# Decay sums masked and exponentiated in the tile they are loaded into, loads issued three ticks sooner

## The chip, the cores and the metric

The kernel runs on one core of a Trainium2 chip, in one launch. The metric is the time of the device for one execution, in microseconds, as a median over runs. TensorE is called PE, VectorE DVE, ScalarE ACT, GpSimd POOL and SyncE SP, as in the profile.

## The reference

One layer for 128 context and 1024 latent tokens, width 1024. Two branches, a Fourier one and a state-space one (SSD), are merged, projected and added to the input. The change touches the SSD branch only, whose core the reference writes like this (once forward and once on the flipped sequence):

```python
xdt = xf * dtf
acs = jnp.cumsum(da, axis=-1)                      # decay sums, within chunks of 128
seg = acs[..., :, None] - acs[..., None, :]
lmat = jnp.exp(jnp.where(tri, seg, -jnp.inf))
y_diag = jnp.einsum("bclgn,bcsgn,bgrcls,bcsgrp->bclgrp", cc, bc, lmat, xdt)
decay_states = jnp.exp(acs[..., -1:] - acs)
chunk_states = jnp.einsum("bcsgn,bgrcs,bcsgrp->bcgrpn", bc, decay_states, xdt)
...
final, states_in = lax.scan(step, s0, (chunk_states, chunk_decay))
y_off = jnp.einsum("bclgn,bcgrpn,bgrcl->bclgrp", cc, states_in, jnp.exp(acs))
y = y_diag + y_off
```

There are 32 heads of 64 channels in 8 groups of 4 heads that share B and C (128 wide), and 9 chunks of 128 tokens: chunk 0 is the context, 1 to 8 are the latents.

## The kernel before

Everything is float32, held transposed (channels on partitions, tokens along the free axis). The large products are done in three matmuls of a high and a low part (`mm3`, L101 to L103); `split` makes these parts: a cast on ACT for the high one (L89), a subtraction on DVE for the low one (L79).

The SSD phase, from about 130 us to 1100 us, is a loop over the 8 groups `g`. A group projects its B, x and C chunks, `GATES[g]` gate chunks and its z chunks, each a `gemm` of 3 token tiles by 8 steps by 3 matmuls of 128x384. Beside them run small steps: transposes, the states and the outputs. The order on PE is written by hand: `at(step, ticks)` puts the next piece of a generator at a tick of a clock, and `gemm` advances this clock by one every 6 matmuls. The other engines' order, SP's queue of DMA issues included, is made by a scheduler from the program and its buffers. Each engine takes its instructions in that order, and a tile of a ring (`tag`, `bufs`) is written again only after all work on its former content.

`states(g, k)` weighs x with DVE (`xw`), splits it into `xhl`, and a yield later runs the `st` matmuls: the first matmul of each needs the high part, the second the low part. For k = -1 the result, the context's final state, goes by ACT's copy `so` (L557) to DRAM; k = 0 to 6 carry the scan on (`st`). `outputs(g, c)` runs once per chunk, in the order 0, 4, 5, 3, 6, 2, 7, 1, 8. SP loads the decay sums of 4 heads and both directions, broadcast to 128 partitions, 512 KB, from `d_acs` (L572) into `ab`; POOL masks them into `e` by two selects (L582, L583), ACT takes 8 exps in `e` (L586), DVE adds the directions (L587). A yield later PE does C times B (`cb`, L590) and DVE multiplies it into `e`; another yield later come the matmuls `po` (from the states) and `y` (L605, from `e`), and DVE adds both into `xs`.

Before, `xhl` and `e` share the tag "e" with three tiles, `ab` and `so` the tag "ab" with two. Loads of an output are six ticks ahead of its `y` in the program, `cb` three; `st` of `k` stands at tick 21 + 3k from its base, and the outputs' clock base is 12 ticks later. In the text, st_3 and xhl_3 mean k = 3, while e_4 or y_0 name the chunk c.

Of the kernel before, what the change touches and what calls it, by code (L numbers as in the profile page):

```python
# [12 lines left out]
F32 = mybir.dt.float32  # L13
F32R = mybir.dt.float32r
AF = mybir.ActivationFunctionType
ALU = mybir.AluOpType
# [46 lines left out]
def tile_step(ctx, tc, a, o):  # L63
# [127 lines left out]
    def at(step, *ticks):  # L191

        for t in ticks:
            events[clock[0] + t].append(step)
# [281 lines left out]
    with pool("sd") as sd, pool("ss") as ss, pool("sx", side="right") as sx:  # L476
# [65 lines left out]
        def states(g, k, xb, bn, sts):  # L542

            cf, cb = (0, 0) if k < 0 else (1 + k, 8 - k)
            xw = ss.tile([P, 2, 256], F32, tag="xw", name=f"xw{g}_{k}", bufs=1)
            xhl = ss.tile([P, 2, 2, 256], F32R, tag="e", name=f"xhl{g}_{k}", bufs=3)
            xh, xl = xhl[:, 0], xhl[:, 1]
            for d, c in ((0, cf), (1, cb)):
                tt(xw[:, d].rearrange("p (j h q) -> p j h q", j=2, h=2), xb[:, c].rearrange("p (j h q) -> p j h q", j=2, h=2),
                   wsv[:, c, d, g, :].rearrange("p (h j) -> p j h", h=2).unsqueeze(3).broadcast_to([P, 2, 2, 64]), ALU.mult)  # L550
            split(xh, xl, xw)
            yield
            ps = gps(f"st{g}_{k}")
            if k < 0:
                mm3(ps, (bn[:, 0, 0], bn[:, 1, 0]), [x.rearrange("p d q -> p (d q)") for x in (xh, xl)], True, True)
                so = ss.tile([P, 1024], F32, tag="ab", name=f"so{g}", bufs=2)[:, 0:512]
                S.copy(so, ps)  # L557
                nc.sync.dma_start(o["sout"][g], so)
                return
            st = sts[0]  # L560
            for d, c in ((0, cf), (1, cb)):
                mm3(ps[:, d * 256 : d * 256 + 256], (bn[:, 0, c], bn[:, 1, c]), (xh[:, d], xl[:, d]), True, True)
            tt(st[:, k + 1].rearrange("p d (h q) -> p d h q", h=4), st[:, k].rearrange("p d (h q) -> p d h q", h=4),
               decv[:, :, g, :, k].unsqueeze(3).broadcast_to([P, 2, 4, 64]), ALU.mult)
            sv = st[:, k + 1].rearrange("p d q -> p (d q)")
            tt(sv, sv, ps, ALU.add)

        def outputs(g, c, bt, ct, xs, xb, st):

            cc = slice(col(c), col(c) + P)  # L570
            ab = ss.tile([P, 2, 4, P], F32, tag="ab", name=f"ab{g}_{c}", bufs=2)
            nc.sync.dma_start(ab.rearrange("p d h l -> p d (h l)"),  # L572
                              d_acs[c].rearrange("(d g q) l -> g d (q l)", d=2, g=NG)[g].partition_broadcast(P))
            if c > 0:

                ea = ss.tile([P, 2, 2, P], F32, tag="ea", name=f"ea{g}_{c}", bufs=3)
                for r0 in range(2):
                    nc.sync.dma_start(ea[r0 * 64 : r0 * 64 + 64].rearrange("p d j l -> p d (j l)"),
                                      d_eac[c].rearrange("(d g h j) l -> g h d (j l)", d=2, g=NG, h=2)[g, r0].partition_broadcast(64))
            e = ss.tile([P, 2, 4, P], F32, tag="e", name=f"e{g}_{c}", bufs=3)  # L580

            G.affine_select(e[:, 0], ab[:, 0], [[0, 4], [1, P]], ALU.is_ge, -1e30, base=0, channel_multiplier=-1)  # L582
            G.affine_select(e[:, 1], ab[:, 1], [[0, 4], [-1, P]], ALU.is_ge, -1e30, base=0, channel_multiplier=1)  # L583
            for d in range(2):
                for h in range(4):
                    act(e[:, d, h], e[:, d, h], AF.Exp, bias=knv[:, c, d, g, h : h + 1])  # L586
# [56 lines left out]
        for g in range(NG):  # L643
# [12 lines left out]
                at(tr_x(g, c0, xs, xb), 11 + i)  # L656
            at(skip(g, xs), 16)
            for k in range(-1, 7):
                at(states(g, k, xb, bn, sts), 17 + 3 * k, 21 + 3 * k)
            conv_silu(C0 + g, 8 + g, ct, f"c{g}")  # L660
            st = ss.tile([P, 8, 2, 256], F32, tag="st", name=f"st{g}")
            sts.append(st)
# [1 line left out]

            for i, c in enumerate((0, 4, 5, 3, 6, 2, 7, 1, 8)):
                t = 20 + 3 * i
                at(outputs(g, c, bt, ct, xs, xb, st), t - 6, t - 3, t)
            done = clock[0] + t
            gate(GATES[g])

# [478 lines left out]
```

## Time and profile before

| | us |
|---|---|
| median of 3 runs | 1739.71 (1739.43 to 1741.41) |
| the profiled execution | 1747.27 |
| its span | 1745.1 |
| PE busy in it | 1711.1 (98%) |
| DVE, ACT, POOL busy | 1094.4, 811.2, 186.5 |

The profiled execution has 2.2 us around its span, and it is 7.6 us longer than the median. The span is cut into instructions by engine; the page gives each engine's busy time, the chain of work that ended last, and groups of instructions by line. A wait of an engine is its idle time ahead of an instruction, put down to what released it. Where the timeline shows `[1.41 <-DVE e L79]`, the engine was idle for 1.41 us and the end of DVE's line 79 on `e` let it go on.

### The profile page before, as it was taken

To read this page: it belongs to the slowest core of one execution; us is meant where nothing else is said; L and a number is where in the kernel's file an instruction comes from. 1 tells how busy PE (TensorE), PEld (TensorE's weight loads), DVE (VectorE), ACT (ScalarE), POOL (GpSimd) and SP (SyncE) were. 2 spreads that over 40 slices of the span, in tenths; PEclk is the share of its full clock that TensorE was granted. 3 is DMA by queue.
4 is the path that set the end of the run, shared out by engine and by line. 5 is a ranking of instruction groups with operands and counts; after the bars stand their busy time and mean duration, and the time that the engine had idled before them with its cause. 6 is when DMAs were issued, how large, how long until landed. Compare 5 with 4: busy or idle time off the path is not lost.

```text
span 1745.1 us, 27930 instructions
## 1 busy us (share of the span) xinstructions
PE 1711.1 (98%) x10728; PEld 1643.9 (94%) x10728; DVE 1094.4 (63%) x1875; ACT 811.2 (46%) x1667; POOL 186.5 (11%) x266
## 2 busy tenths in 40 slices
PE   6999999999999999999899999999999999999998
PEld 4999999999999999999899999999988999999987
DVE  5676866866756757757658668677587424444432
ACT  6445656665565566566466666315333211112221
POOL 0200300300300301301202103301000000000000
PEclk9999999999999999999999999999999999999999
DMA  9233632633523624524525436551066647643432
GB/s 345 78 71 95 157 94 83 150 100 88 151 83 104 146 71 114 144 76 104 122 70 142 103 105 140 195 179 54 3 212 217 221 145 235 220 168 125 160 121 72
DMA packets 110136, 229.63 MB, mean 132 GB/s; under 512 B 20594, under 2 KB 56436, under 8 KB 108340
## 3 DMA queue, kind: packets, MB, share of 16 engines
q1 hardware_dynamic: 108708, 223.14, 42.9%
q0 software_dynamic: 1296, 4.72, 0.7%
q8 instruction: 84, 1.38, 0.3%
q14 instruction: 48, 0.39, 0.1%
HBM read 187.24 MB, written 40.58 MB: 131 GB/s over the span
## 4 chain that ended last, share of the span: by engine, by line
PE 91%; DVE 4%; DMA 3%; ACT 1%; issue 1%; SPq 0%; POOL 0%; DVEq 0%; POOLq 0%; ACTq 0%
PE mm_g L101 5%; PE mm_g L103 5%; PE mm_g L102 5%; PE mm_x L101 4%; PE mm_x L103 4%; PE mm_x L102 4%; PE mm_z L101 3%; PE mm_z L103 3%; PE mm_z L102 3%; PE po L597 3%; PE y L605 2%; PE mm_c L101 2%; PE mm_c L103 2%; PE o L102 2%; PE mm_c L102 2%; PE o L103 2%
## 5 line engine op out<-in xcount | busy, mean ns | idle before, releaser
L73 ACT ACTIVATE e<-e,kwN 128x128 f32<-128x128 f32 x576 | 179.5, 390 | 114.4 <-POOL e L582 108.5
L101 PE MATMUL mm_g<-hT,wh_g 128*128 128x384 f32 x528 | 182.0, 345 | 0.0
L103 PE MATMUL mm_g<-hT,wl_g 128*128 128x384 f32 x528 | 177.9, 337 | 0.0
L102 PE MATMUL mm_g<-hT,wh_g 128*128 128x384 f32 x528 | 177.5, 336 | 0.0
L101 PE MATMUL mm_z<-hT,wh_z 128*128 128x384 f32 x384 | 134.1, 349 | 0.0
L582 POOL TENSOR_SCALAR_AFFINE_SELECT e<-ab 128x512 f32<-128x512 f32 x72 | 50.2, 697 | 779.4 <-PE st L103 662.0
L101 PE MATMUL mm_x<-hT,wh_x 128*128 128x384 f32 x384 | 131.6, 343 | 0.0
L103 PE MATMUL mm_z<-hT,wl_z 128*128 128x384 f32 x384 | 129.8, 338 | 0.0
L102 PE MATMUL mm_z<-hT,wh_z 128*128 128x384 f32 x384 | 129.5, 337 | 0.0
L103 PE MATMUL mm_x<-hT,wl_x 128*128 128x384 f32 x384 | 129.2, 337 | 0.0
L102 PE MATMUL mm_x<-hT,wh_x 128*128 128x384 f32 x384 | 129.0, 336 | 0.0
L101 PEld LDWEIGHTS mm_g<-hT,wh_g 128*128 128x128 f32 x528 | 99.3, 188 | 0.5 <-issue 0.2
L102 PEld LDWEIGHTS mm_g<-hT,wh_g 128*128 128x128 f32 x528 | 99.3, 188 | 0.4
L103 PEld LDWEIGHTS mm_g<-hT,wl_g 128*128 128x128 f32 x528 | 99.1, 188 | 0.0
L101 PEld LDWEIGHTS mm_z<-hT,wh_z 128*128 128x128 f32 x384 | 72.6, 189 | 0.9 <-issue 0.9
L102 PEld LDWEIGHTS mm_z<-hT,wh_z 128*128 128x128 f32 x384 | 72.6, 189 | 0.0
L101 PEld LDWEIGHTS mm_x<-hT,wh_x 128*128 128x128 f32 x384 | 72.1, 188 | 0.3
L103 PEld LDWEIGHTS mm_z<-hT,wl_z 128*128 128x128 f32 x384 | 72.3, 188 | 0.0
L102 PEld LDWEIGHTS mm_x<-hT,wh_x 128*128 128x128 f32 x384 | 72.3, 188 | 0.0
L103 PEld LDWEIGHTS mm_x<-hT,wl_x 128*128 128x128 f32 x384 | 72.1, 188 | 0.0
L597 PE MATMUL po<-ct,st 128*128 128x128 f32 x512 | 67.4, 274 | 0.0
L101 PE MATMUL mm_b<-hT,wh_b 128*128 128x384 f32 x192 | 65.8, 343 | 1.4 <-DVE gt L76 1.4
(419 smaller groups left out, 4746.9 us busy)
## 6 DMA issues: line engine op xcount, KB each, us to landing
ab<-d_acs SPq DMA_DIRECT2D x72, 512.0 KB, 5.9
ea<-d_eac SPq DMA_DIRECT2D x128, 128.0 KB, 3.6
wr_g<-in_w_in SPq DMA_DIRECT2D x24, 512.0 KB, 3.7
yr<-d_y SPq DMA_DIRECT2D x16, 576.0 KB, 4.3
aw<-in_ada_ss SPq DMA_DIRECT2D x8, 1024.0 KB, 10.2
wr_x<-in_w_in SPq DMA_DIRECT2D x16, 512.0 KB, 3.9
wr_z<-in_w_in SPq DMA_DIRECT2D x16, 512.0 KB, 3.6
d_y<-xs SPq DMA_DIRECT2D x16, 512.0 KB, 3.4
```

Of the source, the lines that this page charges most:

```text
L73: S.activation(out, in_, func, bias=bias, scale=scale, **kw)
L101: PE.matmul(ps, lhs[0], rhs[0], start=first, stop=False)
L102: PE.matmul(ps, lhs[0], rhs[1], start=False, stop=False)
L103: PE.matmul(ps, lhs[1], rhs[0], start=False, stop=last)
L582: G.affine_select(e[:, 0], ab[:, 0], [[0, 4], [1, P]], ALU.is_ge, -1e30, base=0, channel_multiplier=-1)
L597: PE.matmul(po[:, (2 * d + j) * P : (2 * d + j + 1) * P], st[:, k, d, j * P : j * P + P], ct[:, cc], start=True, stop=True)
L605: PE.matmul(py[r0 : r0 + 64, j * P : j * P + P], xb[:, c, h * 64 : h * 64 + 64], e[:, 0, h % 2 * 2 + j], start=True, stop=True, tile_posit ...
```

## The change

The separate tile `ab` is gone. The load goes into the `e` tile, where selects and exps then work in place; tag "e" has four tiles, shared by `e` and `so`. `xhl` gets a tag of its own with one tile. `outputs` has one more yield: the load stands nine ticks ahead of `y`, selects and exps six, `cb` three as before. The `st` matmuls stand one tick sooner (20 + 3k). No instruction is added or taken out but the waits; the on-chip memory is the same (five tiles of 4 KB a partition).

```diff
--- before.py
+++ after.py
@@ -543,7 +543,7 @@
 
             cf, cb = (0, 0) if k < 0 else (1 + k, 8 - k)
             xw = ss.tile([P, 2, 256], F32, tag="xw", name=f"xw{g}_{k}", bufs=1)
-            xhl = ss.tile([P, 2, 2, 256], F32R, tag="e", name=f"xhl{g}_{k}", bufs=3)
+            xhl = ss.tile([P, 2, 2, 256], F32R, tag="xhl", name=f"xhl{g}_{k}", bufs=1)
             xh, xl = xhl[:, 0], xhl[:, 1]
             for d, c in ((0, cf), (1, cb)):
                 tt(xw[:, d].rearrange("p (j h q) -> p j h q", j=2, h=2), xb[:, c].rearrange("p (j h q) -> p j h q", j=2, h=2),
@@ -553,7 +553,7 @@
             ps = gps(f"st{g}_{k}")
             if k < 0:
                 mm3(ps, (bn[:, 0, 0], bn[:, 1, 0]), [x.rearrange("p d q -> p (d q)") for x in (xh, xl)], True, True)
-                so = ss.tile([P, 1024], F32, tag="ab", name=f"so{g}", bufs=2)[:, 0:512]
+                so = ss.tile([P, 1024], F32, tag="e", name=f"so{g}", bufs=4)[:, 0:512]
                 S.copy(so, ps)
                 nc.sync.dma_start(o["sout"][g], so)
                 return
@@ -568,8 +568,8 @@
         def outputs(g, c, bt, ct, xs, xb, st):
 
             cc = slice(col(c), col(c) + P)
-            ab = ss.tile([P, 2, 4, P], F32, tag="ab", name=f"ab{g}_{c}", bufs=2)
-            nc.sync.dma_start(ab.rearrange("p d h l -> p d (h l)"),
+            e = ss.tile([P, 2, 4, P], F32, tag="e", name=f"e{g}_{c}", bufs=4)
+            nc.sync.dma_start(e.rearrange("p d h l -> p d (h l)"),
                               d_acs[c].rearrange("(d g q) l -> g d (q l)", d=2, g=NG)[g].partition_broadcast(P))
             if c > 0:
 
@@ -577,10 +577,10 @@
                 for r0 in range(2):
                     nc.sync.dma_start(ea[r0 * 64 : r0 * 64 + 64].rearrange("p d j l -> p d (j l)"),
                                       d_eac[c].rearrange("(d g h j) l -> g h d (j l)", d=2, g=NG, h=2)[g, r0].partition_broadcast(64))
-            e = ss.tile([P, 2, 4, P], F32, tag="e", name=f"e{g}_{c}", bufs=3)
-
-            G.affine_select(e[:, 0], ab[:, 0], [[0, 4], [1, P]], ALU.is_ge, -1e30, base=0, channel_multiplier=-1)
-            G.affine_select(e[:, 1], ab[:, 1], [[0, 4], [-1, P]], ALU.is_ge, -1e30, base=0, channel_multiplier=1)
+            yield
+
+            G.affine_select(e[:, 0], e[:, 0], [[0, 4], [1, P]], ALU.is_ge, -1e30, base=0, channel_multiplier=-1)
+            G.affine_select(e[:, 1], e[:, 1], [[0, 4], [-1, P]], ALU.is_ge, -1e30, base=0, channel_multiplier=1)
             for d in range(2):
                 for h in range(4):
                     act(e[:, d, h], e[:, d, h], AF.Exp, bias=knv[:, c, d, g, h : h + 1])
@@ -656,7 +656,7 @@
                 at(tr_x(g, c0, xs, xb), 11 + i)
             at(skip(g, xs), 16)
             for k in range(-1, 7):
-                at(states(g, k, xb, bn, sts), 17 + 3 * k, 21 + 3 * k)
+                at(states(g, k, xb, bn, sts), 17 + 3 * k, 20 + 3 * k)
             conv_silu(C0 + g, 8 + g, ct, f"c{g}")
             st = ss.tile([P, 8, 2, 256], F32, tag="st", name=f"st{g}")
             sts.append(st)
@@ -664,7 +664,7 @@
 
             for i, c in enumerate((0, 4, 5, 3, 6, 2, 7, 1, 8)):
                 t = 20 + 3 * i
-                at(outputs(g, c, bt, ct, xs, xb, st), t - 6, t - 3, t)
+                at(outputs(g, c, bt, ct, xs, xb, st), t - 9, t - 6, t - 3, t)
             done = clock[0] + t
             gate(GATES[g])
```

The order of instructions moves with it. In the rows that follow, a name is the tile, its group and its index, and a running number; `x8` after a shape means eight in a row.

ACT in group 3, before, from the skip's scaling of `xs3` (L73) to the exps of the group's first output (`gt67`: a gate's tiles, `wh_z`: a weight's split):

```order
L73 ACTIVATE xs3_4944<-xs3_4944,dcol_102 128x1154
L89 CAST xhl3_0_5464<-xw3_0_5463 128x512
L557 COPY so3_5479<-st3_-1_5475 128x512
L73 ACTIVATE gt67_1_5494<-mm_g67_1_5456 128x384
L89 CAST xhl3_1_5498<-xw3_1_5497 128x512
L89 CAST xhl3_2_5532<-xw3_2_5531 128x512
L89 CAST wh_z30_5816<-wr_z30_5817 128x1024
L73 ACTIVATE gt67_2_5543<-mm_g67_2_5503 128x384
L89 CAST xhl3_3_5575<-xw3_3_5574 128x512
L73 ACTIVATE e3_0_5582<-e3_0_5582,kwN_718 128x128 x8
```

and of the changed kernel, to the cast of `xhl3_3`:

```order
L73 ACTIVATE xs3_4917<-xs3_4917,dcol_102 128x1154
L557 COPY so3_5440<-st3_-1_5436 128x512
L89 CAST xhl3_0_5444<-xw3_0_5443 128x512
L73 ACTIVATE gt67_1_5467<-mm_g67_1_5429 128x384
L89 CAST xhl3_1_5480<-xw3_1_5479 128x512
L73 ACTIVATE e3_0_5519<-e3_0_5519,kwN_718 128x128 x8
L89 CAST xhl3_2_5514<-xw3_2_5513 128x512
L73 ACTIVATE e3_4_5579<-e3_4_5579,kwN_718 128x128 x2
L73 ACTIVATE gt67_2_5527<-mm_g67_2_5485 128x384
L73 ACTIVATE e3_4_5579<-e3_4_5579,kwN_718 128x128 x6
L73 ACTIVATE e3_5_5639<-e3_5_5639,kwN_718 128x128 x2
L89 CAST xhl3_3_5559<-xw3_3_5558 128x512
```

The copy `so` and the cast of `xhl3_0` have changed places. The casts of `xhl3_2` and `xhl3_3` stood ahead of all exps; now they stand behind those of `e3_0`, and behind `e3_4` and two of `e3_5`.

SP's queue in group 3, before, from the second gate tile's write (`d_mf<-gt`) on; `wr_` is a weight's load, and in brackets are the semaphores waited for:

```order
L167 DMA d_mf_83<-gt67_1_5494 128x384 [waits DMAHW6_49,Activation_49]
L572 DMA ab3_4_5638<-d_acs_77 128x2x512 [waits DMAHW7_49,DMAHW5_49]
L167 DMA d_mf_83<-gt67_2_5543 128x384 [waits Activation_49]
L572 DMA ab3_5_5704<-d_acs_77 128x2x512 [waits DMAHW4_49,DMAHW1_49,Pool_49]
L178 DMA wr_b4_6240<-in_w_in 128x1024 [waits DMAHW2_49,DVE_49]
L167 DMA d_mf_83<-gt68_0_5619 128x384 [waits DMAHW3_49,Activation_49]
L572 DMA ab3_3_5776<-d_acs_77 128x2x512 [waits DMAHW7_49,Pool_49]
L167 DMA d_mf_83<-gt68_1_5686 128x384 [waits Activation_49]
L572 DMA ab3_6_5851<-d_acs_77 128x2x512 [waits DMAHW6_49,DMAHW1_49,Pool_49]
```

and of the changed kernel, from the same write on:

```order
L167 DMA d_mf_83<-gt67_1_5467 128x384 [waits DMAHW6_49,Activation_49]
L572 DMA e3_4_5579<-d_acs_77 128x2x512 [waits DMAHW7_49]
L572 DMA e3_5_5639<-d_acs_77 128x2x512 [waits PE_49]
L572 DMA e3_3_5704<-d_acs_77 128x2x512 [waits DMAHW5_49,DMAHW1_49]
L167 DMA d_mf_83<-gt67_2_5527 128x384 [waits DMAHW2_49,Activation_49]
L167 DMA d_mf_83<-gt68_0_5596 128x384 [waits DMAHW3_49,Activation_49]
L167 DMA d_mf_83<-gt68_1_5662 128x384 [waits DMAHW4_49,Activation_49]
L572 DMA e3_6_5775<-d_acs_77 128x2x512 [waits DVE_49,PE_49,Pool_49]
L178 DMA wr_b4_6204<-in_w_in 128x1024 [waits DMAHW6_49,DVE_49]
```

The loads of `e3_4`, `e3_5` and `e3_3` now stand one behind the other, directly behind a gate's write. The load of `e3_6`, the fifth of the group, waits for PE, and a weight's load stands right behind it.

ACT in group 5, before, from the cast of `xhl5_5` on, with the `z` tiles (`zt`) between:

```order
L89 CAST xhl5_5_8272<-xw5_5_8271 128x512
L73 ACTIVATE e5_5_8291<-e5_5_8291,kwN_718 128x128 x8
L89 CAST xhl5_6_8336<-xw5_6_8335 128x512
L89 CAST wh_b6_8654<-wr_b6_8655 128x1024
L73 ACTIVATE zt502_8385<-mm_z50_2_8307 128x384
L73 ACTIVATE e5_3_8363<-e5_3_8363,kwN_718 128x128 x8
L73 ACTIVATE e5_6_8438<-e5_6_8438,kwN_718 128x128 x8
```

and of the changed kernel, from the split of a weight to a `z` tile:

```order
L89 CAST wh_z51_8354<-wr_z51_8355 128x1024
L73 ACTIVATE zt501_8226<-mm_z50_1_8163 128x384
L89 CAST xhl5_5_8239<-xw5_5_8238 128x512
L73 ACTIVATE e5_6_8339<-e5_6_8339,kwN_718 128x128 x5
L89 CAST xhl5_6_8302<-xw5_6_8301 128x512
L73 ACTIVATE e5_6_8339<-e5_6_8339,kwN_718 128x128 x3
L73 ACTIVATE zt502_8350<-mm_z50_2_8273 128x384
```

The cast of `xhl5_6` stood ahead of the exps of `e5_6` and of `e5_3`; now five of the exps of `e5_6` precede it.

## Rows read from the trace of the kernel before

**Rows 1.** The page: span, busy time, granted clock in 40 slices, chain by engine.

```profile
span 1745.1 us, 27930 instructions
...
PE 1711.1 (98%) x10728; PEld 1643.9 (94%) x10728; DVE 1094.4 (63%) x1875; ACT 811.2 (46%) x1667; POOL 186.5 (11%) x266
...
PEclk9999999999999999999999999999999999999999
...
PE 91%; DVE 4%; DMA 3%; ACT 1%; issue 1%; SPq 0%; POOL 0%; DVEq 0%; POOLq 0%; ACTq 0%
```

**Rows 2.** Waits of PE: line and releaser, us in total, times, longest.

```profile
PE ps_s L265 <- DVE sq L79: 9.2, 1, 9.2
PE y L605 <- DVE e L79: 8.8, 4, 5.6
```

**Rows 3.** Timeline of `y` on PE: start, us, instruction, [idle before, releaser].

```profile
212.75 0.66 PE L605 MATMUL y<-e,xb 128*64 128x128 f32 x8 [1.41 <-DVE e L79]
...
593.52 0.66 PE L605 MATMUL y<-e,xb 128*64 128x128 f32 x8 [1.25 <-DVE e L79]
...
852.16 1.12 PE L605 MATMUL y<-e,xb 128*64 128x128 f32 x8 [5.60 <-DVE e L79]
...
1083.23 0.66 PE L605 MATMUL y<-e,xb 128*64 128x128 f32 x8 [0.53 <-DVE e L79]
```

**Rows 4.** Timeline of POOL and DVE ahead of the longest wait, group 5.

```profile
845.73 0.63 POOL L582 TENSOR_SCALAR_AFFINE_SELECT e<-ab 128x512 f32<-128x512 f32 x1 [7.87 <-DMA ab<-d_acs]
...
847.09 0.83 DVE L79 TENSOR_TENSOR xs<-xs,ea 128x256 f32<-128x256 f32 x1 [6.56 <-POOL ea L600]
```

**Rows 5.** The chain there: start, us, what.

```profile
837.89 10.64 DMA ab<-d_acs
...
852.03 0.14 issue
```

**Rows 6.** Loads: all of `ab`; one behind a gate's write; one behind a load.

```profile
DMA to landing us min/median/max: 4.8/5.9/8.1
...
ab<-d_acs SPq DMA_DIRECT2D x1, 512.0 KB, 5.9
...
wr_b<-in_w_in SPq DMA_DIRECT2D x1, 512.0 KB, 7.4
```

**Rows 7.** Timeline of ACT, DVE and PE around st_0, group 3.

```profile
547.46 0.61 ACT L89 CAST xhl<-xw 128x512 fp32r<-128x512 f32 x1
547.97 0.58 ACT L557 COPY so<-st_-1_5475 128x512 f32<-128x512 f32 x1
...
548.10 0.69 DVE L79 TENSOR_TENSOR xhl<-xw,xhl 128x512 fp32r<-128x512 f32 x1 [0.30 <-ACT xhl L89]
...
550.16 0.28 PE L101 MATMUL st<-xhl,bn 128*128 128x256 f32 x1
550.28 0.28 PE L102 MATMUL st<-xhl,bn 128*128 128x256 f32 x1
...
550.87 0.34 PE L101 MATMUL mm_g<-hT,wh_g 128*128 128x384 f32 x1
```

**Rows 8.** Timeline of SP's issues in group 3.

```profile
549.83 0.32 SPq L167 DMA_DIRECT2D d_mf<-gt  x1
...
575.96 1.03 SPq L572 DMA_DIRECT2D ab<-d_acs  x1
```

**Rows 9.** Timeline of POOL, ACT and PE at output 1 and 0, group 3.

```profile
562.91 0.64 POOL L582 TENSOR_SCALAR_AFFINE_SELECT e<-ab 128x512 f32<-128x512 f32 x1 [5.67 <-PE st L103]
...
563.58 2.45 ACT L73 ACTIVATE e<-e,kwN 128x128 f32<-128x128 f32 x8 [3.24 <-POOL e L582]
...
560.68 0.38 PE L590 MATMUL cb<-ct,bt 128*128 128x128 f32 x2
```

**Rows 10.** Timeline of PE in group 5: the first `y`, a later `po`.

```profile
819.15 0.55 PE L605 MATMUL y<-e,xb 128*64 128x128 f32 x6
...
829.70 1.05 PE L597 MATMUL po<-ct,st 128*128 128x128 f32 x8
```

## The prediction

> **What bounds the kernel now.** I read the page first. Its busy line shows PE at 98% of the span, and the chain that ended last runs through PE for 91% [rows 1]: time is lost or won only where PE waits. The granted clock reads nine tenths or more of full speed, the 2.4 GHz level, in every slice [rows 1], so a wait costs what it lasts, and PE stays full after this phase, so it is not given back.
>
> Next the waits of PE. Two sums stand out [rows 2]: 9.2 us once, at the start (no part of the change), and 8.8 us in four waits of the `y` matmuls for VectorE on `e`. These are what the change can take away. The timeline of `y` places them [rows 3], all at the sixth of a group's nine outputs: 1.41, 1.25, 5.60 and 0.53 us, in groups 0, 3, 5 and 7. The long one has a cause of its own [rows 4, 5]: a transfer into `ab` stood 10.64 us in the chain, GpSimd's select waited 7.87 us for one, GpSimd's sum of `ea` stood behind that select, VectorE waited 6.56 us for this sum, and the `e` work of the output that PE wanted stood behind VectorE. The usual load takes 4.8 to 8.1 us, median 5.9 [rows 6] (the view leaves out those whose landing it can't assign, the 10.64 among them); a transfer over 10 us is an accident of one execution, I think, while the three short waits come from loads in traffic and look regular.
>
> **The change part by part.** Matmuls, casts, exps, selects and bytes are the same in number; what moves is when, and who waits for a buffer.
>
> *The old waits.* A load now leaves three ticks sooner if its buffer is free. The ring has four tiles, so from the fifth output on the load waits for PE to be through with the `y` four outputs earlier. `y` of one output follows that of the one before by 5.8 us (819.15, and two outputs on 829.70 + 1.05 for `po` [rows 10]), so a late load then leaves some 20 us ahead of its `y`, where the one of group 3 that PE waited for left at 575.96 [rows 8], 17.6 ahead of 593.52. With a median load the short waits go: 1.41 + 1.25 + 0.53 = 3.2 us. In the profiled execution 8.8 could go.
>
> *First new wait: st_0.* `st` moves up a tick, which is six matmuls: 1.03 us. The order on ACT now has the copy `so` ahead of the cast of `xhl_0` (first pair of order rows). Before, in group 3, the cast starts at 547.46 and the copy at 547.97 [rows 7]; after, the copy takes the first place and the cast 547.97 to 548.58. VectorE's subtraction follows 0.03 us behind (547.46 + 0.61, to 548.10) and takes 0.69: 549.30. PE starts about 0.15 behind VectorE, as `y` did (0.14 [rows 5]), so at 549.45. The matmul that needs the low part, the second of st_0, stood at 550.28 [rows 7] and is now due at 549.25. So PE waits 0.20, in all eight groups: 1.6 us. Bounds: nothing (a wait that is new gives no time back), if the small steps overlap, to 0.3 each.
>
> *Second new wait: st_3.* `xhl` had a place in a ring of three, so ACT did the casts far ahead of the exps. Now it has one buffer, a cast waits for the `st` before it, and on ACT the cast xhl_3 stands behind eight exps of output 4 and two of output 5 (groups 2 to 7; first pair of order rows). ACT takes them in that order, so xhl_3 hangs on a load. On SP's queue that load, e_4, stands behind a gate's write (second pair), issued at 549.83 in group 3 for 0.32 us, so it leaves at 550.2 [rows 8]. From its landing: select 0.15 us later (an estimate, one hand-over as from VectorE to PE), the first exp 0.67 after the select, eight exps 2.45 (562.91 to 563.58, and on [rows 9]), the gate's activation about 0.4 (my estimate; the copy of a larger tile takes 0.58 in rows 7), two exps 0.6, cast 0.61, subtraction 0.03 + 0.69, PE 0.15: 5.7 us. st_3 is due where `cb` of output 0 stood, at 560.68 [rows 9], its second matmul at 560.8, or 561.0 with the 0.2 of st_0. With a load of D us the wait is 550.2 + D + 5.7 - 561.0 = D - 5.1. What is D? The quickest took 4.8, one issued right behind a gate's write 5.9, and a 512 KB transfer right behind another 7.4 [rows 6]. Here the load has a write ahead and e_5's load right behind, perhaps e_3's too; the row nearest to it is the 5.9, and I take 6.0: 0.9 us in each of six groups, 5.4 us. Bounds: 0 (D of 4.8) and 2.3 (D of 7.4) each.
>
> By the Trainium skill, DMA: Bandwidth & Descriptors, section "Anatomy of one DMA — SWDGE (gpsimd) path", a transfer costs about 2.0 us plus its bytes at 436 GB/s, which gives 3.2 us for 512 KB (an estimate from that page's fit, made for another issuing path). By this figure st_3 would not wait at all. The trace has no such load under 4.8 us, so I go by the trace.
>
> *Third: st_6.* In groups 5 to 7 the cast xhl_6 stands behind five exps of output 6, before it was ahead of them all (third pair). The load e_6 waits for `y` of output 0. That stood at 819.15 in group 5 [rows 10]; six `st` matmuls now precede it, 0.71 us (550.16 to 550.87 in rows 7), and it takes 0.66 [rows 3], so the load leaves at 820.6 or a little later. From landing: 0.15 + 0.67 + 5 exps at 0.305 (2.45 / 8) = 1.53, then cast, subtraction and PE as above 1.48: 3.83. Due is the second matmul of st_6 where the `po` of output 5 stood, 829.70 + 0.12 [rows 10]. D may be 5.4 at most, 5.3 with some issue time. In groups 2 to 4 only one exp precedes, but a gate's write precedes the load: I put the limit at 5.9. A weight load follows in SP's queue, so again D = 6.0: 0.7 x 3 + 0.1 x 3 = 2.4 us; bounds 0 and 2.1 each.
>
> The other `st` and `y_0` keep 0.1 to 1 us to spare by the same working. VectorE and GpSimd get no new work; in the late outputs GpSimd starts sooner. The extra `yield` moves only the place of the selects.
>
> **The sum.** New: 1.6 + 5.4 + 2.4 = 9.4. Against the profiled execution (span 1745.1, itself 1747.3): 1747.3 + 9.4 - 8.8 = 1747.9. That execution lies 7.6 above the median of 1739.7, of which the 5.6 us wait is probably most. So against the median only the short waits are taken off: 1739.7 + 9.4 - 3.2 = 1745.9, forecast 1746, its own range 1743 to 1750.
>
> **The rivals.**
>
> *Loads sooner pay (faster).* If every execution has a late load somewhere, as the profiled one did, 8.8 us go; if ACT also gets its loads within 5.1 us, only st_0's 1.6 comes: 1739.7 - 8.8 + 1.6 = 1732.5. For it: the four waits are in the trace, and each is a wait for a load's work. Against: three executions agree within 2 us and lie 6 to 8 below the profiled one, and the median load is over 5.1 us. The point from which it decides: D below 5.3. The Trainium skill, DMA: Bandwidth & Descriptors, "Rules for kernel authors", speaks for it: issue a transfer early, compute, and wait for it late. The trace agrees that the old waits come from loads [rows 4, 5]; but here the earlier load also brings its exps ahead of the casts on ACT, which that rule does not weigh.
>
> *The two sides cancel (no change).* The scheduler's order on ACT is right about the loads, D is about 5.2, st_3 costs 0.2 x 6, st_6 0.1 x 3: 1739.7 + 1.6 + 1.2 + 0.3 - 3.2 = 1739.6.
>
> *The loads crowd each other (slower still).* e_4, e_5 and e_3 leave within a microsecond and all land as the 7.4 us one [rows 6]: 2.3 x 6 + 2.1 x 3 + 1.5 x 3 + 1.6 = 26.2 is the worst, 1762.7. At D of 6.7, half way from my 6.0 to there, it is 1.6 x 6 + 1.4 x 3 + 0.8 x 3 + 1.6 = 17.8, less 3.2: 1754.3, which I give this case. For it: nothing in the old order puts three loads in a row, so no row shows it; against: the wait of e_3's load for `so` may part them.
>
> *The change doesn't do what it says.* Loads are no sooner, being paced by `y` four outputs back, the old waits stay, the new ones come: 1739.7 + 9.4 = 1749.1. For it: from the fifth on a load waits for PE (second pair, e3_6). Against: the late outputs gain 2 to 3 us by the count above, more than any of the three short waits.
>
> **How the numbers follow.** Forecast 0.60, cancel 0.18, faster 0.11, crowding 0.06, no sooner 0.05. 0.2% is 3.5 us, about what a measurement can tell from no change. Slower (above 1743.2): most of the forecast's share (0.54), and the last two, 0.65. Same: 0.18 and 0.06 of the forecast's. Faster: 0.11. The range runs from 1737, below which only the faster rival lies, to 1753, above which lies most of the crowding.
>
> **What the next profile shows if I am right.** Among the waits of PE, `st` on VectorE's `xhl`, absent now, with about 20 entries: 0.2 us at st_0 in every group, about 0.9 at st_3 in groups 2 to 7, 0.1 to 0.7 at st_6. The four waits of `y` for `e` gone. On ACT, `xhl` behind exps, and idle time of ACT before those exps that ends at GpSimd's select, itself ended by the load. Clock and busy times of PE unchanged. The forecast is wrong if `st` waits little (loads under 5.3 us), if the waits of `y` come back elsewhere, or if st_1, st_2, st_4 or st_5, where I found room, wait as well.

## The result and the profile after

The changed kernel takes 1766.57 us (median of five runs, 1764.96 to 1768.3), the kernel before 1739.71: the ratio is 1.0154, with a 95% interval of 1.0143 to 1.0166. It is slower, as forecast, but by 26.9 us and not by 6, and outside the range. The profiled execution's span is 1765.5 us.

First the page of the changed kernel: span, busy times, and the chain by engine.

```profile
span 1765.5 us, 27941 instructions
...
PE 1721.6 (98%) x10728; PEld 1648.0 (93%) x10728; DVE 1092.5 (62%) x1875; ACT 807.7 (46%) x1667; POOL 193.3 (11%) x266
...
PE 83%; DMA 6%; DVE 5%; ACT 2%; issue 2%; SPq 1%; POOL 1%; POOLq 0%; DVEq 0%; ACTq 0%
```

Against [rows 1], PE is busy for 10.5 us more with the same 10728 matmuls: so some of them took longer, and not all of the loss is listed as waiting: part is a lower clock, part a wait that hides in the time of the matmul before it (both below). DMA has gone from 3 to 6% of the chain.

The waits of PE in the changed kernel (in total, times, longest):

```profile
PE st L101 <- ACT xhl L89: 7.9, 7, 1.6
PE st L102 <- DVE xhl L79: 5.5, 10, 0.7
...
PE y L605 <- issue: 3.0, 5, 1.9
PE y L605 <- ACT e L73: 1.9, 2, 1.2
...
PE y L605 <- DVE e L79: 0.2, 1, 0.2
```

The waits of `st` are the new ones that were forecast. But they stand at other places: at st_2 in groups 0, 1 and 7 and at st_3 in groups 1 to 7, none at st_6; and the first matmul of a state waits for ACT's cast as well as the second for DVE's subtraction. The waits of `y` [rows 2, 3] have not gone: 8.8 us have become 5.1, at the fourth to eighth output of a group. The longest, 1.9 us, is new (group 4); at the sixth output of groups 3 and 7 a wait is still there (0.7 and 1.2 us, where it was 1.25 and 0.53).

How one such place comes about shows best in group 4, in the order of the work. SP's issues (start, time of the issue itself, count), with the gate's write that is ahead of them:

```profile
689.84 0.32 SPq L167 DMA_DIRECT2D d_mf<-gt  x1
690.20 0.98 SPq L572 DMA_DIRECT2D e<-d_acs  x2
...
691.82 1.49 SPq L572 DMA_DIRECT2D e<-d_acs  x1
```

Three loads of 512 KB, e_4, e_5 and e_3, leave within 1.6 us. POOL's selects of these three tell when each has come, as POOL waits for it:

```profile
697.68 0.78 POOL L582 TENSOR_SCALAR_AFFINE_SELECT e<-e 128x512 f32<-128x512 f32 x1 [4.42 <-DMA e<-d_acs]
...
700.82 0.64 POOL L582 TENSOR_SCALAR_AFFINE_SELECT e<-e 128x512 f32<-128x512 f32 x1 [1.77 <-DMA e<-d_acs]
...
703.34 0.94 POOL L582 TENSOR_SCALAR_AFFINE_SELECT e<-e 128x512 f32<-128x512 f32 x1 [1.30 <-DMA e<-d_acs]
```

From issue to select 7.5 us, then about 10.1 (the second issue is at about 690.7), then 11.5, where [rows 6] had 5.9 as the median of all and 4.8 as the least. It is much the same in each of groups 2 to 7: 6.0 to 7.6 us for e_4, 8.6 to 10.1 for e_5, 9.3 to 11.5 for e_3. ACT and DVE stand behind these selects:

```profile
701.48 0.69 ACT L73 ACTIVATE e<-e,kwN 128x128 f32<-128x128 f32 x2 [0.17 <-POOL e L582]
702.08 0.60 ACT L89 CAST xhl<-xw 128x512 fp32r<-128x512 f32 x1
...
701.41 1.17 DVE L79 TENSOR_TENSOR e<-e 128x512 f32<-128x512 f32 x1 [3.44 <-ACT e L73]
702.50 0.67 DVE L79 TENSOR_TENSOR st<-st,st 128x512 f32<-128x512 f32 x1
703.10 0.68 DVE L79 TENSOR_TENSOR xhl<-xw,xhl 128x512 fp32r<-128x512 f32 x1
```

The cast xhl_3 has two exps of output 5 ahead of it on ACT, and these have the second load. On DVE the subtraction has the add of output 4 ahead of it, which waited 3.44 us for exps. So PE, in the timeline of the same place:

```profile
700.83 0.34 PE L103 MATMUL mm_g<-hT,wl_g 128*128 128x384 f32 x1
702.74 0.39 PE L101 MATMUL st<-xhl,bn 128*128 128x256 f32 x1 [1.57 <-ACT xhl L89]
703.84 0.58 PE L102 MATMUL st<-xhl,bn 128*128 128x256 f32 x1 [0.71 <-DVE xhl L79]
704.21 0.41 PE L103 MATMUL st<-xhl,bn 128*128 128x256 f32 x1
704.43 0.41 PE L101 MATMUL st<-xhl,bn 128*128 128x256 f32 x1
...
705.81 0.52 PE L102 MATMUL mm_g<-hT,wh_g 128*128 128x384 f32 x1
```

st_3 was due at 701.0 and starts at 702.74, and its second matmul at 703.84. Behind the wait the `st` matmuls are 0.22 us apart, where they were 0.12 apart in [rows 7], and those of the gemm take 0.52 where they took 0.34. The windows of that stretch give the granted clock (the last column but two):

```profile
core 0: us, PE busy (x) PEld busy (x) DVE busy (x) ACT busy (x) POOL busy (x), PEclk, DMA share, GB/s
...
698.00:702.60 4.60, 3.16 (x19) 2.84 (x17) 1.19 (x2) 3.94 (x13) 2.27 (x4) 1.00 0.50 180
...
704.10:706.00 1.90, 1.90 (x9) 1.90 (x10) 1.90 (x4) 1.89 (x7) 1.21 (x2) 0.50 0.16 57
706.00:708.00 2.00, 2.00 (x11) 2.00 (x10) 2.00 (x4) 1.97 (x6) 0.00 (x0) 0.75 0.12 44
```

After the wait PE runs at 0.50, the 1.2 GHz level, and comes back within 706 to 708. To price a place I took the start of the same gemm matmul in both traces, ahead of it and behind: before 686.38 and 690.47, after 698.91 and 707.23. The lag grows from 12.53 to 16.76: 4.2 us, of which 2.7 are the waits (701.0 to 702.74, and 703.84 less 702.86), and 1.5 the slow stretch. By the same comparison st_2 and st_3 together cost 3.7, 4.1, 3.8, 1.5, 4.2, 1.4, 4.3 and 1.5 us in groups 0 to 7: 24.5 us. The granted clock reads 0.50 behind the waits in groups 0, 2, 4 and 6, and 1.00 behind those of groups 1, 3, 5 and 7.

st_4 and st_5 of groups 5 and 7 lose 0.7 us more in each group, which no line of waits lists. The sum then comes near: 1.6 (st_0, below) + 24.5 + 1.4 + 5.1 (new waits of `y`) - 4.5 (old ones, in a profile of the kernel before without the 5.6 us wait, the control e8) = 28.1, for 26.9 between the medians and 27.1 between the spans of these two profiles (1765.5 and 1738.4).

### The profile page after: what moved, and what is told of

Its sections match the earlier page's. It is cut to its first block, busy times and chain, and to the rows that moved or that the text cites. A ratio compares the mean times of both kernels' runs of the same rounds, so it can differ in the third digit from the quotient of the medians.

```text
span 1765.5 us, 27941 instructions
## 1 busy us (share of the span) xinstructions
PE 1721.6 (98%) x10728; PEld 1648.0 (93%) x10728; DVE 1092.5 (62%) x1875; ACT 807.7 (46%) x1667; POOL 193.3 (11%) x266
## 4 chain that ended last, share of the span: by engine, by line
PE 83%; DMA 6%; DVE 5%; ACT 2%; issue 2%; SPq 1%; POOL 1%; POOLq 0%; DVEq 0%; ACTq 0%
DMA e<-d_acs 5%; PE mm_x L101 3%; PE mm_x L103 3%; PE mm_x L102 3%; PE mm_g L101 3%; PE mm_g L103 3%; PE mm_g L102 3%; PE mm_z L101 3%; PE mm_z L102 3%; PE mm_z L103 3%; PE po L597 3%; PE y L605 2%; PE mm_c L101 2%; PE mm_c L102 2%; PE o L102 2%; PE o L103 2%
## 5 line engine op out<-in xcount | busy, mean ns | idle before, releaser
L73 ACT ACTIVATE e<-e,kwN 128x128 f32<-128x128 f32 x576 | 180.4, 390 | 160.9 <-POOL e L582 158.3
L582 POOL TENSOR_SCALAR_AFFINE_SELECT e<-e 128x512 f32<-128x512 f32 x72 | 53.2, 738 | 803.6 <-DMA e<-d_acs 740.8
L79 DVE TENSOR_TENSOR e<-e 128x512 f32<-128x512 f32 x72 | 52.8, 733 | 43.2 <-ACT e L73 27.1
```

Of the source, the lines that this page charges most:

```text
L73: S.activation(out, in_, func, bias=bias, scale=scale, **kw)
L79: V.tensor_tensor(out, in0, in1, op=op)
L582: G.affine_select(e[:, 0], e[:, 0], [[0, 4], [1, P]], ALU.is_ge, -1e30, base=0, channel_multiplier=-1)
```

## The experiments

The theory at this point, called A: one `xhl` buffer puts the casts on ACT, and the subtractions on DVE, behind work on late loads; and the four-tile ring lets a group's first loads leave together, so that they are late. Rivals: B, loads that leave sooner do the harm in themselves; C, the tick of `st` does it. Later runs add D, the single tile does it whatever the loads take; E, loads that leave sooner and straight into `e` crowd everything, wherever the casts stand; F, the waits follow from the loads' lateness, however far apart the `st` are.

**The load six ticks ahead again.**

```diff
-                at(outputs(g, c, bt, ct, xs, xb, st), t - 9, t - 6, t - 3, t)
+                at(outputs(g, c, bt, ct, xs, xb, st), t - 6, t - 6, t - 3, t)
```

> The changed kernel with the load back at six ticks ahead of y, in one step with the selects; tiles and rings as changed. Theory A (the one buffer of xhl puts its cast on ACT behind exps whose loads crowd each other): ACT and SP keep the order of the changed kernel, the waits of st stay, 1766 us within 3. Rival B (loads that leave sooner do the harm): about 1745 or less.

1767.38 us, ratio 1.0168 (1.0153 to 1.0184) to the kernel before: as the changed kernel. The order on SP and ACT is the same but for a few rows. "Three ticks sooner" is thus not what moves the loads: the scheduler issues a load when its tile is free, and the ring decides that. B in the form "the load's tick" is out. In its profile the granted clock falls to 0.50 behind one wait of this phase (group 3) and not behind four, and its span is 1763.5 us for 1765.5.

**`st` at its old tick.**

```diff
-                at(states(g, k, xb, bn, sts), 17 + 3 * k, 20 + 3 * k)
+                at(states(g, k, xb, bn, sts), 17 + 3 * k, 21 + 3 * k)
```

> The changed kernel with the st matmuls back at tick 21 + 3k. Theory A: every st has a tick (1.03 us) more, so the 0.2 us at st_0 goes in eight groups and up to 1.03 us of each of some nine waits at st_2 and st_3: 1766.6 - 1.6 - 8 = 1757 us. Rival C (the tick alone is the cause): back to 1740 us or under.

1750.31 us, 1.0066 (1.0049 to 1.0083): 16 us less than changed, where A said 9.6, and 12 more than before, where C said none. Its waits of PE on `st`; the list has none of `y`:

```profile
PE st L102 <- DVE xhl L79: 9.0, 8, 1.7
...
PE st L101 <- ACT xhl L89: 1.8, 3, 0.9
```

The tick matters, but not as slack: the listed waits of `st` fell only from 13.4 to 10.8 us. What went beside are the 5.1 us of `y`, st_0's 1.6, and slow stretches: 0.50 is read behind one wait (group 1), not behind four. The clock is the smaller part of the 16 us, since e1's profile has one slow stretch too and is only 2.0 us shorter than the changed kernel's. By the comparison of starts, against the control e8, st_2 and st_3 cost 12.9 us here, and st_4 to st_6 of groups 2 to 4 another 4.3.

**The kernel before with one `xhl` tile of its own.**

```diff
-            xhl = ss.tile([P, 2, 2, 256], F32R, tag="e", name=f"xhl{g}_{k}", bufs=3)
+            xhl = ss.tile([P, 2, 2, 256], F32R, tag="xhl", name=f"xhl{g}_{k}", bufs=1)
...
-    gq = right.enter_context(pool("gq", 6, side="right"))
+    gq = right.enter_context(pool("gq", 5, side="right"))
```

> The kernel before, with its ab and e rings and its ticks, but xhl in a tag of its own with one tile (the ring of gate tiles gq goes from six to five to make room). Theory A: the cast xhl_3 stands behind ten exps again, st_3 waits for it in groups 2 to 7, about 1 to 2 us each, 1747 to 1752 us. Rivals B and C (early loads, the tick): no change, 1740 us within 2.

1749.49 us, 1.0064 (1.0049 to 1.0079), as A said, and C is out for these 11 us. The ticks and the `ab` ring are those of the kernel before, and the waits of `st` are there:

```profile
PE st L102 <- DVE xhl L79: 5.8, 10, 1.1
...
PE st L101 <- ACT xhl L89: 2.5, 4, 1.5
```

So the edit of the single tile makes some 11 us. The loads didn't stay as they were, though: e_4 and e_5 of group 3 now leave within 1.6 us and are selected 5.6 and 7.0 us later, where they left 5 us apart. B, loads that leave sooner, isn't excluded by this run. (Five gate tiles cost nothing: e8 below.)

**All five tiles in one ring.** The changed kernel, with `xhl` back beside `e` and `so`:

```diff
-            xhl = ss.tile([P, 2, 2, 256], F32R, tag="xhl", name=f"xhl{g}_{k}", bufs=1)
+            xhl = ss.tile([P, 2, 2, 256], F32R, tag="e", name=f"xhl{g}_{k}", bufs=5)
...
-                so = ss.tile([P, 1024], F32, tag="e", name=f"so{g}", bufs=4)[:, 0:512]
+                so = ss.tile([P, 1024], F32, tag="e", name=f"so{g}", bufs=5)[:, 0:512]
...
-            e = ss.tile([P, 2, 4, P], F32, tag="e", name=f"e{g}_{c}", bufs=4)
+            e = ss.tile([P, 2, 4, P], F32, tag="e", name=f"e{g}_{c}", bufs=5)
```

> The changed kernel with xhl back in the ring with e and so, now five tiles for all three (the same memory); load nine ticks ahead, in place, st a tick sooner. Theory A: the casts stand ahead of the exps again, only the 0.2 us at st_0 is left (1.6 us in all), the old waits of y go: 1738 us (1735 to 1743). Rivals B and C: 1755 us or more.

1753.42 us, 1.0084 (1.0069 to 1.0099). A missed by 15 us, and it is 1.6 us under what B and C said. The waits of `st` went as it said (one of 0.3 is left), but others took their place:

```profile
PE y L605 <- issue: 10.5, 10, 3.5
...
PE y L605 <- DVE e L79: 0.5, 1, 0.5
...
PE st L102 <- DVE xhl L79: 0.3, 1, 0.3
```

Six of a group's nine loads now leave in pairs, 0.5 to 1.6 us apart (0 and 4, 6 and 2, 7 and 1). POOL's select of a later output waits 3.19 us for one of them ahead of the sum of `ea`, DVE's `xs` waits 4.21 us for that sum (336.84 and 341.85 in its timeline), and the `e` work for `y` stands behind it: the mechanism of [rows 4]. So early loads do cost where they come together, also with the casts out of their way.

**Half the bytes.**

```diff
-            nc.sync.dma_start(e.rearrange("p d h l -> p d (h l)"),
-                              d_acs[c].rearrange("(d g q) l -> g d (q l)", d=2, g=NG)[g].partition_broadcast(P))
+            nc.sync.dma_start(e[:, 0].rearrange("p h l -> p (h l)"),
+                              d_acs[c].rearrange("(d g q) l -> g d (q l)", d=2, g=NG)[g, 0].partition_broadcast(P))
...
-            G.affine_select(e[:, 0], e[:, 0], [[0, 4], [1, P]], ALU.is_ge, -1e30, base=0, channel_multiplier=-1)
-            G.affine_select(e[:, 1], e[:, 1], [[0, 4], [-1, P]], ALU.is_ge, -1e30, base=0, channel_multiplier=1)
+            G.affine_select(e[:, 1], e[:, 0], [[0, 4], [1, P]], ALU.is_ge, -1e30, base=0, channel_multiplier=-1)
+            G.affine_select(e[:, 0], e[:, 0], [[0, 4], [1, P]], ALU.is_ge, -1e30, base=0, channel_multiplier=-1)
...
-                    act(e[:, d, h], e[:, d, h], AF.Exp, bias=knv[:, c, d, g, h : h + 1])
+                    act(e[:, d, h], e[:, d, h], AF.Exp, bias=knv[:, c, 0, g, h : h + 1])
```

> The changed kernel, but each load of decay sums brings the forward direction alone (256 KB for 512), which then stands in for both directions in selects and exps; as many selects, exps and loads as before, and the backward term of y is not the reference's. Theory A (a cast waits behind exps whose loads crowd each other): the load of output 5's sums in a group's first burst lands in 6 us or less where it took 8.4 to 10, and the waits of st at st_2 and st_3, some 22 us in all, fall by more than half: 1752 us (1748 to 1757). Rival D (the waits come from the single buffer alone, whatever the loads take): 1763 us or more.

1742.52 us, 1.0016 (1.0007 to 1.0024): 24 us less than the changed kernel with the same rings, ticks and casts behind still more exps (xhl_3 behind six of output 5), and 5 us below the range that A gave. What is left of the waits, and the loads' time from issue to landing:

```profile
PE st L102 <- DVE xhl L79: 2.3, 6, 0.6
...
DMA to landing us min/median/max: 3.0/3.8/5.2
```

The changed kernel's line of the same view reads 5.0/6.0/9.7. So the single tile costs by way of the loads' time: with quicker loads its price is some 3 us, st_0's 1.6 among them. Half the bytes make every load quicker, one by itself too, so this run doesn't show how much is the crowding. Rival D (the tile alone, whatever the loads take) is out.

**Two `xhl` tiles, and with `st` at the old tick.**

```diff
-            xhl = ss.tile([P, 2, 2, 256], F32R, tag="xhl", name=f"xhl{g}_{k}", bufs=1)
+            xhl = ss.tile([P, 2, 2, 256], F32R, tag="xhl", name=f"xhl{g}_{k}", bufs=2)
...
-    gq = right.enter_context(pool("gq", 6, side="right"))
+    gq = right.enter_context(pool("gq", 5, side="right"))
```

> The changed kernel with two xhl tiles in place of one (the ring of gate tiles gq goes from six to five to make room). Theory A: each cast stands one state further ahead, xhl_3 before any exp of output 5, so what is left is st_0's 0.2 in eight groups and some tenths at st_2 and st_3: 1741 us (1738 to 1746). Rival C (the tick) or rival E (loads in place crowd everything): 1755 or more.

And the same with the old tick:

```diff
-                at(states(g, k, xb, bn, sts), 17 + 3 * k, 20 + 3 * k)
+                at(states(g, k, xb, bn, sts), 17 + 3 * k, 21 + 3 * k)
```

> As the one before, and the st matmuls at tick 21 + 3k as in the kernel before. Theory A: no wait of st above some tenths, and the three short waits of y gone: 1736 us (1734 to 1740), 0.1 to 0.2% faster than the kernel before. Rival E: 1745 or more.

1759.71 us, 1.0115 (1.0098 to 1.0131), and 1746.26, 1.0038 (1.0027 to 1.005). A missed both, by 19 and 10 us, and both lie where E had them. In e6 the waits of `st` shrank, and `y` of a group's first output waits instead:

```profile
PE y L605 <- DVE e L79: 9.1, 6, 1.7
PE st L102 <- DVE xhl L79: 3.6, 6, 1.4
```

In group 2 DVE stands idle for 3.0 us for a cast that is still behind exps of output 4, and then does the adds of outputs 4 and 5 ahead of the product that the first `y` needs. In e7 no wait of `st` is listed, and `y` waits for 6.3 us in all, most of it again at the first output. A second tile moves the place, not the cause.

**A control: the kernel before with five gate tiles.**

```diff
-    gq = right.enter_context(pool("gq", 6, side="right"))
+    gq = right.enter_context(pool("gq", 5, side="right"))
```

> The kernel before with five gate tiles in the ring gq in place of six and nothing else, as a control for the other kernels that have five. All theories: no change, 1738.5 us within 1.5. If it is slower by 2 us or more, that much comes off what the others lose.

1740.44 us, 1.0000 (0.9988 to 1.0012). The room taken for the others costs nothing. Its profile also shows the typical waits of `y`: 1.07, 1.21, 1.72 and 0.52 us, 4.5 in all, without the one of 5.6 in [rows 3].

**A third `ab` tile in the kernel before.** Casts stay ahead of the exps; loads may leave sooner.

```diff
-            ab = ss.tile([P, 2, 4, P], F32, tag="ab", name=f"ab{g}_{c}", bufs=2)
+            ab = ss.tile([P, 2, 4, P], F32, tag="ab", name=f"ab{g}_{c}", bufs=3)
...
-                so = ss.tile([P, 1024], F32, tag="ab", name=f"so{g}", bufs=2)[:, 0:512]
+                so = ss.tile([P, 1024], F32, tag="ab", name=f"so{g}", bufs=3)[:, 0:512]
...
-    gq = right.enter_context(pool("gq", 6, side="right"))
+    gq = right.enter_context(pool("gq", 5, side="right"))
```

> The kernel before with a third ab tile (and five gate tiles in gq to make room): loads may leave sooner, but ab, e and xhl keep rings of their own as before, and the casts stay ahead of the exps on ACT. Theory A: sooner loads alone do no harm, the waits of y for late loads go (4.5 us in the control's profile), no wait of st: 1735.5 us (1734 to 1738). Rival E (any sooner load crowds the others and costs): 1742 or more.

1735.93 us, 0.9981 (0.997 to 0.9992), as A said. PE has no wait for `st` or `y`. The loads did leave sooner (e_5 of group 3 at 551.1, in the control at 557.4). Rival E in the form "any sooner load costs" is out, and B with it.

They were no quicker than in the changed kernel. But POOL's selects wait for them far less often. The lines give the idle time in total, which includes the stretches between groups, and how many of the 72 selects waited; here:

```profile
  DMA ab<-d_acs: 13.8, 5
...
DMA to landing us min/median/max: 5.0/5.9/9.8
```

and in the changed kernel:

```profile
  DMA e<-d_acs: 740.8, 59
```

So loads of up to 10 us do no harm by themselves: here most have landed when their turn comes, and in the changed kernel the queues stand and wait for them.

**The tick alone, in the kernel before.**

```diff
-                at(states(g, k, xb, bn, sts), 17 + 3 * k, 21 + 3 * k)
+                at(states(g, k, xb, bn, sts), 17 + 3 * k, 20 + 3 * k)
```

> The kernel before with the st matmuls a tick sooner (20 + 3k) and nothing else. Theory A, and the prediction's first step: PE waits 0.20 us at st_0 in eight groups, or nothing where the order on ACT is another: 1739.5 to 1741.5 us. Rival C (the tick is what costs): 1750 or more.

1735.74 us, 0.9977 (0.9965 to 0.999): faster, which no theory said. Rival C is out in the kernel before. The waits of PE, from the top of the list, with no `st` and no `y`:

```profile
PE ps_s L265 <- DVE sq L79: 9.5, 2, 8.8
PE ps_t L298 <- DVE arow L293: 3.3, 2, 2.8
PE tb L519 <- DVE bt L76: 1.6, 1, 1.6
PE mm_b L101 <- DVE gt L76: 1.4, 1, 1.4
```

The earlier `st` lets a group's later loads leave sooner (that of output 2 in group 3 at 572.6, and at 576.1 in the control), which fits with the waits of `y` being gone; that it is the reason is my reading and not shown.

**`st` three ticks later.**

```diff
-                at(states(g, k, xb, bn, sts), 17 + 3 * k, 20 + 3 * k)
+                at(states(g, k, xb, bn, sts), 17 + 3 * k, 23 + 3 * k)
```

> The changed kernel with the st matmuls three ticks later (23 + 3k). Theory A: each cast has 3.1 us more, more than the longest wait of st for it (2.3 us) in the changed kernel, so the clock isn't let down either: 1738 us (1735 to 1744). If waits of y for VectorE take their place, the loads' lateness sits in VectorE's queue as well: 1745 to 1755.

1789.52 us, 1.0286 (1.0259 to 1.0312): A missed by over 50 us, in sign too. The waits of `st` stay, and a new one comes, for the low part of a z weight, whose subtraction on DVE now has a state's subtraction ahead of it, and that a cast behind an exp whose load is late:

```profile
PE mm_z L103 <- DVE wl_z L79: 15.1, 3, 5.3
PE st L101 <- ACT xhl L89: 9.9, 9, 2.0
...
PE st L102 <- DVE xhl L79: 4.6, 12, 0.7
```

My reading of slack was wrong: with one tile the cast of a state starts only when the `st` before it is done, so a later tick moves both ends and gives nothing. One tick later is 16 us faster (e2) and three are 23 us slower, so a tick does more than shift the `st`; what it changes in the orders wasn't followed.

**Three tiles for `e` and `so`, two for `xhl`, `st` at the old tick.**

```diff
-            xhl = ss.tile([P, 2, 2, 256], F32R, tag="xhl", name=f"xhl{g}_{k}", bufs=1)
+            xhl = ss.tile([P, 2, 2, 256], F32R, tag="xhl", name=f"xhl{g}_{k}", bufs=2)
...
-                so = ss.tile([P, 1024], F32, tag="e", name=f"so{g}", bufs=4)[:, 0:512]
+                so = ss.tile([P, 1024], F32, tag="e", name=f"so{g}", bufs=3)[:, 0:512]
...
-            e = ss.tile([P, 2, 4, P], F32, tag="e", name=f"e{g}_{c}", bufs=4)
+            e = ss.tile([P, 2, 4, P], F32, tag="e", name=f"e{g}_{c}", bufs=3)
...
-                at(states(g, k, xb, bn, sts), 17 + 3 * k, 20 + 3 * k)
+                at(states(g, k, xb, bn, sts), 17 + 3 * k, 21 + 3 * k)
```

> The changed kernel with the five tiles shared out anew: three for e and so, two for xhl, and st at 21 + 3k. A group's first burst is two loads in place of three (the third waits for a y). Theory A: the second load of the burst lands in about 7 us where it took 9, waits of st and y are a few tenths, 1740 us (1737 to 1745). Rival E: 1746 or more, as with four e tiles.

1739.25 us, 0.9996 (0.998 to 1.0013): no change against the kernel before, 7 us better than e7 with its four `e` tiles. E is right for four tiles filled in place, then, and wrong for three. No wait of `st` is listed, and 2.9 us of `y`, the longest 1.4. With three, the third load of a burst waits for a `y`; the slowest load of the view took 7.9 us (9.7 in the changed kernel).

**`st` four ticks apart.** This tests the corrected reading.

```diff
-                at(states(g, k, xb, bn, sts), 17 + 3 * k, 20 + 3 * k)
+                at(states(g, k, xb, bn, sts), 17 + 3 * k, 20 + 4 * k)
```

> The changed kernel with the st matmuls four ticks apart in place of three (20 + 4k), all else as changed, the one xhl buffer too. Theory A in its corrected form: with one buffer a cast can only stand between two st, so what counts is their distance and not their tick; with four ticks (4.2 us) in place of three the cast and the subtraction fit behind the late exps of output 5, the waits of st at st_2 and st_3 (24 us with the slow stretches behind them) fall by two thirds or more: 1748 us (1742 to 1753). Rival F (the waits follow from the loads' lateness whatever the distance): 1760 or more.

1750.57 us, 1.0056 (1.0037 to 1.0076): 16 us less than the changed kernel, with its single tile and its burst. F is out. The waits of `st` fell to a third, and `y` of the second output now waits in seven groups:

```profile
PE y L605 <- DVE e L79: 3.9, 7, 0.9
PE st L102 <- DVE xhl L79: 3.5, 5, 1.3
...
PE st L101 <- ACT xhl L89: 0.9, 1, 0.9
```

**Both faster edits together**, the third `ab` tile of e9 and the tick of e10:

```diff
-            ab = ss.tile([P, 2, 4, P], F32, tag="ab", name=f"ab{g}_{c}", bufs=2)
+            ab = ss.tile([P, 2, 4, P], F32, tag="ab", name=f"ab{g}_{c}", bufs=3)
...
-                at(states(g, k, xb, bn, sts), 17 + 3 * k, 21 + 3 * k)
+                at(states(g, k, xb, bn, sts), 17 + 3 * k, 20 + 3 * k)
```

> The kernel before with a third ab tile (five gate tiles in gq) and the st matmuls a tick sooner, the two edits that were each faster alone. Neither left a wait of PE in this phase, so together they give no more: 1735.8 us within 1.5. If it is 1734 or less, one of them still had a wait that the other takes.

1737.71 us, 0.9987 (0.9978 to 0.9997): no better than either alone, and 0.4 us above the range stated. PE has no wait for `st` or `y` in any of the three. Against both kernels, 1739.7 and 1766.6, all three are faster, by 0.1 to 0.2% against the kernel before; the tick alone (e10) is the simplest.

## Why the prediction was wrong

*Direction and first step: right.* New waits of `st` outweigh the old ones of `y`. The casts do stand behind exps that hang on loads, as the forecast had it from the order rows. st_0 was given 0.20 us in eight groups. In group 3 of the changed kernel:

```profile
559.95 0.28 PE L101 MATMUL st<-xhl,bn 128*128 128x256 f32 x1
560.16 0.39 PE L102 MATMUL st<-xhl,bn 128*128 128x256 f32 x1
560.38 0.28 PE L103 MATMUL st<-xhl,bn 128*128 128x256 f32 x1
```

The steps are 0.21 and 0.22 us where [rows 7] have 0.12: together 0.20 more, and by the comparison of gemm starts it is 0.19 to 0.32 in each of the eight groups. No line of waits lists it, since it is hidden in the time of the matmul before.

*Second step, st_3: the one that failed.* 5.4 us were forecast, and st_2 and st_3 cost 24.5. The text has st_3 wait for "D - 5.1", with D the load of e_4 alone, and takes the two exps of output 5 ahead of the cast as 0.6 us of work. They have a load of their own, the next in the burst: 10.1 us to its select in group 4, against 7.5 for e_4 and the 6.0 that I took for D. I had the row for a load behind a load, 7.4 us [rows 6], and used it for a bound on e_4 only, not for e_5; and three in a row I put into a rival with 6%. That rival had the mechanism, and its 1754 the wrong size; its worst case, 1762.7, is still below the 1766.6 measured. That the loads' time is the price is shown: with half the bytes 24 of the 27 us go (e5). That it counts how many leave together is shown beside two `xhl` tiles only: three `e` tiles in place of four take 7 us off (e12 against e7). The figure of 3.2 us per load from the Trainium skill (DMA: Bandwidth & Descriptors, "Anatomy of one DMA — SWDGE (gpsimd) path") is for another issuing path, as the prediction says; the least here was 4.8 us, and in the burst of group 4 the loads took 2.3 to 3.6 times that estimate to their selects.

*"The other `st` keep 0.1 to 1 us": failed.* In groups 0 and 1 st_2 waits 1.3 us for the cast alone, as xhl_2 has an exp of output 4 ahead of it and four loads leave close together. I looked at the queue of ACT but not at that of DVE, where the adds of outputs 4 and 5 stand ahead of a subtraction; e6 and e4 show DVE carrying the same lateness to `y`.

*"A wait costs what it lasts": failed.* In group 4 the 2.7 us of waits cost 1.5 more at the 1.2 GHz level. This is a small part of the loss: e1 has one such stretch in place of four and loses as much. The trace of before had shown it, had I read the clock behind its longest wait: 0.50 of full speed from 852.2 to 856.

*Third step, st_6: failed.* 2.4 us were forecast, none is listed. In group 5 the load took 5.9 us to its select and the subtraction ended just in time, as st_4 and st_5 ahead of it had lost 0.3 and 0.4 us of their own (hidden, as at st_0).

*The old waits: failed.* 3.2 us were to go, and 5.1 us of `y` waits are there; the forecast that late outputs have more ahead is right for their loads (e_2 of group 3 leaves 20.9 us ahead of its `y`, 17.6 before), but other work still stands ahead in DVE's queue: in group 7 a sum of `ea` that DVE waits for, in group 4 the split of a weight. That the 5.60 us wait was an accident was right: the control e8 has 1.72 us in its place.

*What the forecast of rivals missed.* The Trainium skill's rule to issue early and wait late (the same page, "Rules for kernel authors") holds where the ring is added to (e9, faster), and not where the tile is taken from a ring that kept casts ahead (the changed kernel, slower, with loads that leave sooner too). Settled by the runs: what costs is work that PE needs, standing in a queue behind work on a load that hasn't landed. The single tile puts it there (11 us in e3, 3 with quicker loads in e5); four or five tiles filled in place do it too, by way of `y`, with more tiles for `xhl` (15 us in e4, 20 in e6, 7 in e7); without either nothing is lost (e9, e12). Open is how the 27 us divide between the two, how a tick of `st` comes to change the order so much (e2, e11), and why e4's loads come in pairs.

## What to carry to other kernels

When a change takes a buffer from a ring, read the order that the scheduler makes of it on every engine that works in a fixed order, and for each instruction ahead of the one that matters ask which load it waits for, not how long it works. Price a load by its place in a burst: in group 4 the second and third of three took 10 and 11.5 us to their selects, where the quickest load landed in 5. Then ask how long before its turn it leaves: loads of up to 10 us cost nothing where they had that time (e9). An extra tick in a program is no slack if both ends of the interval move with it.

## What the runs showed of the hardware

- Three broadcast loads of 512 KB issued within 1.6 us by SP were selected 7.5, 10.1 and 11.5 us after their issue; the quickest such load of a run landed in 4.8 to 5.0 us, and loads of 256 KB landed in 3.0 to 5.2 (e5).
- Behind the waits in groups 0, 2, 4 and 6 the granted clock of the changed kernel read 0.50 for some 3 us; behind the waits of under 1 us in groups 3, 5 and 7 it stayed at 1.00. It did so too in group 1, behind waits of 1.31 and 0.41 us, and in group 6 of e3, behind waits of 1.55 and 0.71; and it fell in group 0 behind 1.32 and 0.34: what decides this the runs don't show.
